# Expert weights in 2 MiB blocks: eight buffers of 4096 columns in place of sixteen of 2048

## The chip, the cores and the metric

The kernel runs on one core of a Trainium2 chip. The metric is the device time of one execution in microseconds (us), as the median of the runs shown. Shares, waits and durations come from one profiled execution, whose own time stands beside its span.

## What is computed

Two consecutive layers of a decoder trunk work on 256 tokens of width 1024, all in float32. Layer 0 has a hybrid mixer (gated linear attention beside sparse attention) and a dense SwiGLU. Layer 1 has a Mamba-2 mixer and eight SwiGLU experts of hidden width 3584, of which each token goes through the best two. A final norm follows. The part that most of the time goes to is this:

```python
def swiglu(h, w_gu, w_down):
    g, u = jnp.split(h @ w_gu, 2, axis=-1)
    return (jax.nn.silu(g) * u) @ w_down

def moe_ffn(h, router, w_gu, w_down):
    logits = (h @ router).astype(jnp.float32)
    top_val, top_idx = lax.top_k(logits, TOP_K)          # TOP_K = 2, N_EXPERTS = 8
    weights = jax.nn.softmax(top_val, axis=-1)
    gate = jnp.sum(jax.nn.one_hot(top_idx, N_EXPERTS) * weights[..., None], axis=-2)
    out = jnp.zeros(h.shape, jnp.float32)
    for e in range(N_EXPERTS):
        out = out + gate[..., e:e + 1] * swiglu(h, w_gu[e], w_down[e])
    return out
```

Every norm in front of a block is scaled and shifted by a projection of a vector `c` (1024 to 3072 columns per block). The weights of those projections are the "mod" weights below.

## The kernel before

**Stages.** From 0 to about 195 us the hybrid mixer runs, to about 375 us the dense SwiGLU, to about 610 us the Mamba-2 mixer, and from there to the end the experts. All matrix products of the first three stages are float32 products made of three: each block of weights is split into a high part (`wh`, ScalarE, line 252) and a low part (`wl`, VectorE, line 253), and TensorE multiplies high by high, high by low and low by high (lines 267 to 269). The split parts live in a ring of four slots of 1024 columns (pool `hl`). The mod weights of the next layers (`ssm_mod`, `moe_mod`) are multiplied and summed on VectorE (line 281, writing `junk`), as work between the splits of the dense stage.

**Loads.** All weights come through `load`: it takes a tile `raw` of 128 x 2048 float32 (1 MiB, 8192 bytes in a row per partition) and issues one DMA from the SP queue. The tiles come from pools that grow as room becomes free: six buffers at first, nine from the dense stage on, sixteen in the expert stage. A DMA into a buffer waits until the last reader of the block before is done, and the order on SP is fixed, so a DMA that waits holds up those behind it. The program has eight semaphores for SP's DMAs, and the ninth DMA waits until the first has landed: at most eight are under way. These waits are named DMAHW0 to DMAHW7 in the order of the program.

**Experts.** Each of the eight experts takes 42 blocks of 1 MiB, 352 MB in all. An expert's tokens are gathered into groups of 32 slots, three groups for the experts at even places and two for those at odd places, since the eight experts are worked through in an order that puts larger and smaller ones in turn. Its 3584 hidden columns are cut into chunks of 1024, 1024, 1024 and 512. For a chunk `gate_up` streams the weights `e_gu` (or `e_gl` for the short chunk) past the gathered tokens `gx`: one block of 1 MiB is one slice `k` of the contraction, and per group four matmuls of 32 rows by 512 columns run side by side on TensorE's column strips. Then SiLU (ScalarE, line 1470) and a product (VectorE, line 1471) write `sg`, `turn_a` transposes it to `at` (TensorE, line 1337), and `down` multiplies `at` by the blocks of `e_dn`. `scaled` multiplies an expert's result by its gate and splits it (`gate` on VectorE, `yh` on ScalarE, `yl` on VectorE, lines 1363 to 1365), and `scatter` adds it to the tokens (TensorE, line 1375). `gather` and `back` prepare the next two experts in between: `gather` is a generator that the loop advances by a step after the third yield of `gate_up` and after each SiLU.

**What sets the order.** The instructions are written in program order and then placed by a list scheduler, which estimates durations, puts what it expects to be ready first, and gives out the buffers. So another size of block also moves instructions on the compute engines, in the stages whose source lines are not touched too.

Of the kernel before, what the change touches and what calls it, by code (L numbers as in the profile page):

```python
# [8 lines left out]
F32 = mybir.dt.float32  # L9
# [7 lines left out]
D, T, KD = 1024, 256, 8  # L17
# [3 lines left out]
FE = 3584  # L21
NE = 8
# [81 lines left out]
def _layout(v):  # L104

    f = {k: np.asarray(a) for k, a in v.items()}
# [18 lines left out]
    for m in MODS:  # L125
# [51 lines left out]
    o["e_gu"] = eg.reshape(NE, 8, 128, 2, FE)[..., :3072].reshape(NE, 8, 128, 2, 3, 4, 256).transpose(  # L177
        0, 4, 1, 2, 5, 3, 6).reshape(NE, 3, 8, 128, 2, 1024)
    o["e_gl"] = eg.reshape(NE, 4, 2, 128, 2, FE)[..., 3072:].reshape(NE, 4, 2, 128, 2, 4, 128).transpose(
        0, 1, 3, 2, 5, 4, 6).reshape(NE, 4, 128, 2, 1024)  # L180
    o["e_dn"] = f["moe_w_down"][0].reshape(NE, 14, 2, 128, D).transpose(0, 1, 3, 2, 4)
# [4 lines left out]
def trunk_kernel(ctx: ExitStack, tc: tile.TileContext, d: dict, out: bass.AP):  # L186
    nc = tc.nc
# [5 lines left out]
    raw_p = ctx.enter_context(tc.tile_pool(name="raw", bufs=6))  # L193
# [27 lines left out]
    raws, hls = [(raw_p, 6)], []  # L221
# [11 lines left out]

    def load(ap):

        ap = ap.rearrange("p a b c -> p (a b c)") if len(ap.shape) == 4 else ap.rearrange("p a b -> p (a b)")
        r = ring("raw").tile([128, 2048], F32, name="raw")
        nc.sync.dma_start(r[:, :ap.shape[1]], ap)
        return r[:, :ap.shape[1]]
# [660 lines left out]
    raws.append((ctx.enter_context(tc.tile_pool(name="raw2", bufs=3, side="right")), 3))  # L900
# [286 lines left out]
    raws.append((ctx.enter_context(tc.tile_pool(name="raw3", bufs=7, side="right")), 7))  # L1187
    with ExitStack() as mx:
# [124 lines left out]
        def gate_up(e, c):  # L1313

            w = CHUNKS[c] // 2
            ps = [pbank("pa") for _ in range(NGS[e])]
            n = 512 // w
            for i in range(KD // n):
                blk = load(weights(e, d["e_gu"], c, i) if n == 1 else weights(e, d["e_gl"], i))
                for q in range(n):  # L1320
                    k = n * i + q
                    for r in range(NGS[e]):
                        strips(ps[r], [(gx[:, e % 4, k, r * NS:(r + 1) * NS],
                                        blk[:, (4 * q + j) * w:(4 * q + j + 1) * w]) for j in range(4)],
                               k == 0, k == KD - 1)
                yield ps
# [14 lines left out]
        def down(e, c, at, py):  # L1341
            m = CHUNKS[c] // 512
            n = NGS[e]

            def part(blk, f, r, h):
                j, f_ = divmod(f, m)
                o_ = f % 2 * D + h * 512
                return at[:, r * m + f_, 32 * j:32 * j + 32], blk[:, o_:o_ + 512]

            for i in range(2 * m):  # L1350
                blk = load(weights(e, d["e_dn"], 4 * c + i))
                for f in (2 * i, 2 * i + 1):
                    strips(py[0], [part(blk, f, r, h) for r in range(2) for h in range(2)],
                           c == 0 and f == 0, c == 3 and f == 4 * m - 1)
                if n == 3:
                    strips(py[1], [part(blk, f, 2, h) for f in (2 * i, 2 * i + 1) for h in range(2)],
                           c == 0 and i == 0, c == 3 and i == 2 * m - 1)
# [140 lines left out]
        def final():  # L1498
            xf = ring("raw").tile([128, 2048], F32, name="raw").rearrange("p (b n) -> p b n", b=2)
# [22 lines left out]
        with tc.If(nmax > 0):  # L1522
# [10 lines left out]
            with tc.For_i(0, NE, 1) as e:  # L1533
                for base in (0, 128):
# [23 lines left out]
                    for f0 in range(0, FE, 512):  # L1558
                        c, h_ = divmod(f0, 1024)
                        pgu = [pbank("pa") for _ in range(2)]  # L1560
                        for k in range(KD):
                            if c < 3:
                                r = load(d["e_gu"][bass.ds(e, 1), c, k].rearrange("a p k n -> p a k n"))
                                rk_ = r.rearrange("p (j u n) -> p u j n", j=4, u=2)[:, :, h_ // 256:h_ // 256 + 2]
                            else:
                                if k % 2 == 0:
                                    r = load(d["e_gl"][bass.ds(e, 1), k // 2].rearrange("a p k n -> p a k n"))
                                rk_ = r.rearrange("p (k j u n) -> p k u j n", k=2, j=4, u=2)[:, k % 2]
                            for u in range(2):
                                PE.matmul(pgu[u].rearrange("p (j n) -> p j n", n=rk_.shape[3]), g2[:, k], rk_[:, u],  # L1570
                                          start=k == 0, stop=k == KD - 1)
# [11 lines left out]
                        for f in range(4):  # L1583
                            if f % 2 == 0:
                                r = load(d["e_dn"][bass.ds(e, 1), f0 // 256 + f // 2].rearrange("a p k n -> p a k n"))
                            for n in range(2):
                                PE.matmul(py[n], at[:, f * 128:(f + 1) * 128],
                                          r[:, (f % 2) * D + n * 512:(f % 2) * D + n * 512 + 512],
                                          start=f0 == 0 and f == 0, stop=f0 == FE - 512 and f == 3)
# [28 lines left out]
```

## Time and profile before

| | us |
|---|---|
| median of 3 runs | 1457.8 (1455.94 to 1460.75) |
| profiled execution, its time | 1462.21 |
| its span, first to last instruction | 1460.3 |
| TensorE busy | 1416.4 (97% of the span) |
| VectorE busy | 562.3 (39%) |
| ScalarE busy | 436.2 (30%) |
| matmuls of the expert stage (line 1303), busy | 507.7 and 253.0 |
| bytes read from HBM | 490.70 MB |

The profile's page has the busy time of each engine, the span in 40 slices with the DMA rate in each, the chain of work that ended last, and the costliest groups of instructions with what ended the idle time before them. The rest is asked of the trace: waits by engine, windows, the chain in order of time, and a timeline of single instructions. A busy TensorE is not proof that it computes all the time, since the ends of its matmuls are modelled. What shows that it waits are the starts.

### The profile page before, as it was taken

What the parts mean: (1) busy time and instruction counts of PE and PEld (TensorE: products, weight loads), DVE (VectorE), ACT (ScalarE), POOL (GpSimd) and SP (SyncE); (2) the same over time, 40 slices, a digit from 0 to 9 for tenths busy, and PEclk for the clock granted to TensorE, in tenths of its full rate; (3) what the DMA queues carried; (4) which work ended last, traced back from release to release, by engine and by line L of the source; (5) the groups of instructions that cost most, each with busy time, mean ns of one, the idle gap of its engine ahead of it and who ended that gap; (6) DMA issues with size and microseconds to landing.
All of it is one profiled execution on the core that took longest, in us unless ns stands there. A gap on an engine that the chain in (4) does not pass through costs nothing.

```text
span 1460.3 us, 28550 instructions
## 1 busy us (share of the span) xinstructions
PE 1416.4 (97%) x12241; PEld 807.4 (55%) x12241; DVE 562.3 (39%) x1100; ACT 436.2 (30%) x854; POOL 5.3 (0%) x13
## 2 busy tenths in 40 slices
PE   6999999999999999999999999999999999999995
PEld 6866799999799987633433333333334333333331
DVE  7898688875678778511010011010100110100102
ACT  5577554444567685211100011000001000000001
POOL 0000000000000000000000000000000000000000
PEclk9999999999999999899999999999999999999998
DMA  9876788985544434799899999999999999999994
GB/s 383 347 287 251 298 297 333 366 312 210 229 145 160 158 116 144 288 362 369 336 410 421 419 420 420 419 421 420 420 420 420 420 421 420 420 420 420 420 420 161
DMA packets 68964, 493.66 MB, mean 338 GB/s; under 512 B 7648, under 2 KB 7904, under 8 KB 9568
## 3 DMA queue, kind: packets, MB, share of 16 engines
q1 hardware_dynamic: 68832, 491.77, 84.1%
q8 instruction: 98, 1.61, 0.4%
q14 instruction: 34, 0.28, 0.1%
HBM read 490.70 MB, written 1.05 MB: 337 GB/s over the span
## 4 chain that ended last, share of the span: by engine, by line
PE 93%; DVE 2%; DMA 2%; ACT 2%; issue 0%; SPq 0%; ACTq 0%; DVEq 0%
PE pa L1303 33%; PE pb L1303 16%; PE pa L267 7%; PE pa L268 7%; PE pa L269 7%; PE pb L268 3%; PE pb L269 3%; PE pb L267 3%; PE pc L1375 2%; PE pc L1337 1%; PE pc L1261 1%; DMA raw<-in_e_dn_dram 1%; PE pb L702 1%; DMA raw<-in_hyb_mod_dram 1%; ACT wh L252 1%; PE pa L732 1%
## 5 line engine op out<-in xcount | busy, mean ns | idle before, releaser
L1303 PE MATMUL pa<-raw,gx 128*32 128x512 f32 (+1 forms) x5120 | 507.7, 541 | 0.0
L1303 PEld LDWEIGHTS pa<-raw,gx 128*32 128x32 f32 x5120 | 166.9, 110 | 301.1 <-issue 262.0
L1303 PE MATMUL pb<-raw,at 128*32 128x512 f32 x2240 | 253.0, 594 | 2.2 <-DMA raw<-in_e_dn_dram 2.2
L1471 DVE TENSOR_TENSOR sg<-sg,pa 128x256 f32<-128x256 f32 (+1 forms) x80 | 31.0, 388 | 476.4 <-ACT sg L1470 474.7
L253 DVE TENSOR_TENSOR wl<-raw,wh 128x1024 fp32r<-128x1024 f32 (+1 forms) x155 | 185.5, 1205 | 58.4 <-ACT wh L252 58.2
L252 ACT CAST wh<-raw 128x1024 fp32r<-128x1024 f32 (+1 forms) x155 | 159.1, 1036 | 122.6 <-PE pb L268 52.9
L1303 PEld LDWEIGHTS pb<-raw,at 128*32 128x32 f32 x2240 | 70.5, 110 | 154.1 <-issue 144.2
L1470 ACT ACTIVATE sg<-pa 128x256 f32<-128x256 f32 (+1 forms) x80 | 28.6, 358 | 347.5 <-PE pa L1303 347.5
L267 PE MATMUL pa<-hh,wh 128*128 128x256 f32 (+1 forms) x392 | 113.4, 292 | 1.3 <-ACT hh L380 0.6
L268 PE MATMUL pa<-hl,wh 128*128 128x256 f32 (+1 forms) x392 | 112.7, 288 | 0.8 <-DVE hl L386 0.8
L269 PE MATMUL pa<-hh,wl 128*128 128x256 f32 (+1 forms) x392 | 112.6, 289 | 0.0
L267 PE MATMUL pb<-hh,wh 128*128 128x256 f32 (+1 forms) x360 | 101.9, 284 | 1.9 <-ACT hh L380 1.9
L268 PE MATMUL pb<-hl,wh 128*128 128x256 f32 (+1 forms) x360 | 102.5, 285 | 0.1
L269 PE MATMUL pb<-hh,wl 128*128 128x256 f32 (+1 forms) x360 | 102.2, 284 | 0.0
L1338 ACT COPY at<-pc 128x512 f32<-128x512 f32 (+2 forms) x32 | 17.5, 546 | 262.3 <-PE pb L1303 134.9
L281 DVE SCALAR_TENSOR_TENSOR junk<-raw,scb 128x1024 bf16<-128x1024 f32 x72 | 87.8, 1219 | 1.6 <-DMA raw<-in_hyb_mod_dram 1.0
L267 PEld LDWEIGHTS pa<-hh,wh 128*128 128x128 f32 (+1 forms) x392 | 74.9, 192 | 5.0 <-ACT wh L252 1.5
L268 PEld LDWEIGHTS pa<-hl,wh 128*128 128x128 f32 (+1 forms) x392 | 75.5, 193 | 2.1 <-DVE hl L386 0.9
L269 PEld LDWEIGHTS pa<-hh,wl 128*128 128x128 f32 (+1 forms) x392 | 75.3, 192 | 0.8 <-DVE gu L629 0.3
L267 PEld LDWEIGHTS pb<-hh,wh 128*128 128x128 f32 (+1 forms) x360 | 68.4, 190 | 2.9 <-ACT hh L380 2.1
L268 PEld LDWEIGHTS pb<-hl,wh 128*128 128x128 f32 (+1 forms) x360 | 68.7, 191 | 1.0 <-DVE hl L386 0.5
L269 PEld LDWEIGHTS pb<-hh,wl 128*128 128x128 f32 (+1 forms) x360 | 68.7, 191 | 0.3
(423 smaller groups left out, 1467.2 us busy)
## 6 DMA issues: line engine op xcount, KB each, us to landing
raw<-in_e_gu_dram SPq DMA_DIRECT2D x192, 1024.0 KB, 18.4
raw<-in_e_dn_dram SPq DMA_DIRECT2D x112, 1024.0 KB, 19.7
raw<-in_e_gl_dram SPq DMA_DIRECT2D x32, 1024.0 KB, 18.3
raw<-in_d_gu_dram SPq DMA_DIRECT2D x22, 1024.0 KB, 7.6
raw<-in_s_in_dram SPq DMA_DIRECT2D x20, 1024.0 KB, 4.8
raw<-in_hyb_mod_dram SPq DMA_DIRECT2D x12, 1024.0 KB, 9.6
raw<-in_ssm_mod_dram SPq DMA_DIRECT2D x12, 1024.0 KB, 6.6
raw<-in_d_dn_dram SPq DMA_DIRECT2D x11, 1024.0 KB, 7.3
```

Of the source, the lines that this page charges most:

```text
L252: hi_last[0] = S.copy(hi[:, :n], r)
L253: lo_last[0] = V.tensor_sub(lo[:, :n], r, hi[:, :n].bitcast(F32))
L267: PE.matmul(ps, a[0], b[0], start=start, stop=False, **kw)
L268: PE.matmul(ps, a[0], b[1], start=False, stop=False, **kw)
L269: return PE.matmul(ps, a[1], b[0], start=False, stop=stop, **kw)
L281: V.scalar_tensor_tensor(jk, r[:, q * D:(q + 1) * D], 1.0, scb, op0=OP.mult, op1=OP.mult, accum_out=macc[m][:, 2 * j + q:2 * j + q + 1])
L702: PE.matmul(pss[g], qbT[g * 64:(g + 1) * 64, r, q * 128:(q + 1) * 128], kT[g * 64:(g + 1) * 64, :, :n], start=True, stop=True)
L1303: up_last[0] = PE.matmul(ps[32 * j:32 * j + 32, :rhs.shape[1]], lhs, rhs, start=start, stop=stop)
L1338: (V.tensor_copy if i else S.copy)(at[:, i:i + n].rearrange("p a n -> p (a n)"), pt_[:, :n * 128])
L1375: PE.matmul(pso[b], at_place[e, q][:, h, b], p[:, q], start=i == 0, stop=i == 2 * n - 1)
L1470: last = act(sg[:, r, :w], pg[r][:, :w], AF.Silu)
L1471: V.tensor_mul(sg[:, r, :w], sg[:, r, :w], pg[r][:, w:2 * w])
```

## The change

The expert weights are laid out in blocks of 2 MiB: two slices of the contraction in one block of `e_gu`, four in one of `e_gl`, four row blocks in one of `e_dn`. A partition's row is 16384 bytes and contiguous. The buffers hold 4096 columns: three at first, four from the dense stage on, eight in the expert stage. Loads of up to 2048 columns, which is every load outside the experts, take half a buffer each: the first of two takes a new tile and the second takes its other half. The loops of `gate_up` and `down` walk the larger blocks in the same order of arithmetic, and `gate_up` yields after every second slice instead of each. The branch for tokens beyond the slots, which this input doesn't take, is changed alike and left out here.

```diff
     eg = f["moe_w_gu"][0]

-    o["e_gu"] = eg.reshape(NE, 8, 128, 2, FE)[..., :3072].reshape(NE, 8, 128, 2, 3, 4, 256).transpose(
-        0, 4, 1, 2, 5, 3, 6).reshape(NE, 3, 8, 128, 2, 1024)
-    o["e_gl"] = eg.reshape(NE, 4, 2, 128, 2, FE)[..., 3072:].reshape(NE, 4, 2, 128, 2, 4, 128).transpose(
-        0, 1, 3, 2, 5, 4, 6).reshape(NE, 4, 128, 2, 1024)
-    o["e_dn"] = f["moe_w_down"][0].reshape(NE, 14, 2, 128, D).transpose(0, 1, 3, 2, 4)
+    o["e_gu"] = eg.reshape(NE, 4, 2, 128, 2, FE)[..., :3072].reshape(NE, 4, 2, 128, 2, 3, 4, 256).transpose(
+        0, 5, 1, 3, 2, 6, 4, 7).reshape(NE, 3, 4, 128, 2, 2048)
+    o["e_gl"] = eg.reshape(NE, 2, 4, 128, 2, FE)[..., 3072:].reshape(NE, 2, 4, 128, 2, 4, 128).transpose(
+        0, 1, 3, 2, 5, 4, 6).reshape(NE, 2, 128, 4, 1024)
+    o["e_dn"] = f["moe_w_down"][0].reshape(NE, 7, 4, 128, D).transpose(0, 1, 3, 2, 4)
...
-    raw_p = ctx.enter_context(tc.tile_pool(name="raw", bufs=6))
+    raw_p = ctx.enter_context(tc.tile_pool(name="raw", bufs=3))
...
-    raws, hls = [(raw_p, 6)], []
+    raws, hls = [(raw_p, 3)], []
...
+    half = [None]
+
     def load(ap):

         ap = ap.rearrange("p a b c -> p (a b c)") if len(ap.shape) == 4 else ap.rearrange("p a b -> p (a b)")
-        r = ring("raw").tile([128, 2048], F32, name="raw")
-        nc.sync.dma_start(r[:, :ap.shape[1]], ap)
-        return r[:, :ap.shape[1]]
+        n = ap.shape[1]
+        if n <= 2048 and half[0] is not None:
+            r, half[0] = half[0], None
+        else:
+            r = ring("raw").tile([128, 4096], F32, name="raw")
+            half[0] = r[:, 2048:] if n <= 2048 else None
+        nc.sync.dma_start(r[:, :n], ap)
+        return r[:, :n]
...
-    raws.append((ctx.enter_context(tc.tile_pool(name="raw2", bufs=3, side="right")), 3))
+    raws.append((ctx.enter_context(tc.tile_pool(name="raw2", bufs=1, side="right")), 1))
...
-    raws.append((ctx.enter_context(tc.tile_pool(name="raw3", bufs=7, side="right")), 7))
+    raws.append((ctx.enter_context(tc.tile_pool(name="raw3", bufs=4, side="right")), 4))
...
-            n = 512 // w
+            n = 1024 // w
             for i in range(KD // n):
-                blk = load(weights(e, d["e_gu"], c, i) if n == 1 else weights(e, d["e_gl"], i))
+                blk = load(weights(e, d["e_gu"], c, i) if n == 2 else weights(e, d["e_gl"], i))
...
-                yield ps
+                    if k % 2 and k < KD - 1:
+                        yield ps
+            yield ps
...
-                o_ = f % 2 * D + h * 512
+                o_ = f % 4 * D + h * 512
                 return at[:, r * m + f_, 32 * j:32 * j + 32], blk[:, o_:o_ + 512]

-            for i in range(2 * m):
-                blk = load(weights(e, d["e_dn"], 4 * c + i))
-                for f in (2 * i, 2 * i + 1):
+            for i in range(m):
+                blk = load(weights(e, d["e_dn"], 2 * c + i))
+                for f in range(4 * i, 4 * i + 4):
                     strips(py[0], [part(blk, f, r, h) for r in range(2) for h in range(2)],
                            c == 0 and f == 0, c == 3 and f == 4 * m - 1)
-                if n == 3:
-                    strips(py[1], [part(blk, f, 2, h) for f in (2 * i, 2 * i + 1) for h in range(2)],
-                           c == 0 and i == 0, c == 3 and i == 2 * m - 1)
+                    if n == 3 and f % 2:
+                        strips(py[1], [part(blk, g, 2, h) for g in (f - 1, f) for h in range(2)],
+                               c == 0 and f == 1, c == 3 and f == 4 * m - 1)
```

In the dense stage on SP, around the seventh load of `ssm_mod` (a number behind a name tells one tile from another; what a row waits for is in brackets). Before, every load has a tile of its own:

```order
L238 DMA raw_2659<-in_d_gu_dram 128x2048 [waits DMAHW5_49]
L238 DMA raw_2725<-in_ssm_mod_dram 128x2048 [waits DMAHW6_49,DVE_49]
L238 DMA raw_2731<-in_ssm_mod_dram 128x2048 [waits DMAHW7_49,DMAHW3_49,DVE_49]
L238 DMA raw_2737<-in_ssm_mod_dram 128x2048 [waits DMAHW0_49,DVE_49,Activation_49]
L238 DMA raw_2743<-in_d_dn_dram 128x2048 [waits DMAHW4_49,DVE_49]
L238 DMA raw_2778<-in_d_gu_dram 128x2048 [waits DMAHW2_49,DVE_49,Activation_49]
L238 DMA raw_2845<-in_d_gu_dram 128x2048 [waits DMAHW6_49,DVE_49]
```

Now the same stretch has a tile for two loads, and the first of the two carries the wait for its buffer:

```order
L245 DMA raw_2527<-in_d_dn_dram 128x2048 [waits DVE_49]
L245 DMA raw_2527<-in_d_gu_dram 128x2048
L245 DMA raw_2699<-in_ssm_mod_dram 128x2048 [waits DMAHW2_49,DMAHW5_49,DMAHW1_49,DVE_49]
L245 DMA raw_2628<-in_d_gu_dram 128x2048 [waits DMAHW6_49,DVE_49,Activation_49]
L245 DMA raw_2628<-in_ssm_mod_dram 128x2048 [waits DMAHW7_49]
L245 DMA raw_2699<-in_ssm_mod_dram 128x2048 [waits DMAHW0_49]
L245 DMA raw_2710<-in_d_dn_dram 128x2048 [waits DVE_49]
L245 DMA raw_2710<-in_d_gu_dram 128x2048
L245 DMA raw_2811<-in_d_gu_dram 128x2048 [waits DMAHW3_49,DMAHW4_49,DVE_49,Activation_49]
```

The seventh load of `ssm_mod` (raw_2725 before, the second half of raw_2628 now) shares a buffer with a block of `d_gu`, and the eighth and ninth share raw_2699.

On VectorE in the same stretch, before, where `wl` is a split, `junk` the work on the mod weights, and `a` and `al` belong to the dense SwiGLU:

```order
L253 TENSOR_TENSOR wl_2409<-raw_2406,wh_2408 128x1024
L281 SCALAR_TENSOR_TENSOR junk_2727,mac_ssm_79<-raw_2725,scb_70 128x1024
L915 TENSOR_TENSOR a_2347<-sg_2345,pb_2286 128x256
L253 TENSOR_TENSOR wl_2437<-raw_2406,wh_2436 128x1024
L919 TENSOR_TENSOR al_2350<-a_2347,ah_2349 128x256
L281 SCALAR_TENSOR_TENSOR junk_2729,mac_ssm_79<-raw_2725,scb_70 128x1024
L253 TENSOR_TENSOR wl_2476<-raw_2473,wh_2475 128x1024
L281 SCALAR_TENSOR_TENSOR junk_2733,mac_ssm_79<-raw_2731,scb_70 128x1024
L253 TENSOR_TENSOR wl_2504<-raw_2473,wh_2503 128x1024
L281 SCALAR_TENSOR_TENSOR junk_2735,mac_ssm_79<-raw_2731,scb_70 128x1024
L253 TENSOR_TENSOR wl_2560<-raw_2557,wh_2559 128x1024
L281 SCALAR_TENSOR_TENSOR junk_2739,mac_ssm_79<-raw_2737,scb_70 128x1024
```

And now, beginning with the splits of the block of `d_dn` (raw_2527; raw_2557 before):

```order
L260 TENSOR_TENSOR wl_2530<-raw_2527,wh_2529 128x1024
L260 TENSOR_TENSOR wl_2546<-raw_2527,wh_2545 128x1024
L922 TENSOR_TENSOR a_2438<-sg_2436,pb_2378 128x256
L288 SCALAR_TENSOR_TENSOR junk_2695,mac_ssm_79<-raw_2628,scb_70 128x1024
L926 TENSOR_TENSOR al_2441<-a_2438,ah_2440 128x256
L288 SCALAR_TENSOR_TENSOR junk_2697,mac_ssm_79<-raw_2628,scb_70 128x1024
L260 TENSOR_TENSOR wl_2564<-raw_2527,wh_2563 128x1024
L288 SCALAR_TENSOR_TENSOR junk_2701,mac_ssm_79<-raw_2699,scb_70 128x1024
L922 TENSOR_TENSOR a_2505<-sg_2503,pb_2444 128x256
L260 TENSOR_TENSOR wl_2592<-raw_2527,wh_2591 128x1024
L926 TENSOR_TENSOR al_2508<-a_2505,ah_2507 128x256
L288 SCALAR_TENSOR_TENSOR junk_2703,mac_ssm_79<-raw_2699,scb_70 128x1024
```

The work on the seventh load stood between the two splits of a block of `d_gu` two blocks earlier, and stands now behind the two splits of the block of `d_dn`.

On TensorE in the expert stage, where an odd expert's last `down` ends and its first `scatter` begins, before:

```order
L1303 MATMUL pb<-raw,at 32x512 x16
L1303 MATMUL pa<-raw,gx 32x512
L1375 MATMUL pc<-yh,stT 128x512
L1375 MATMUL pc<-yl,stT 128x512
L1375 MATMUL pc<-yh,stT 128x512
L1375 MATMUL pc<-yl,stT 128x512
```

and now:

```order
L1310 MATMUL pb<-raw,at 32x512 x16
L1384 MATMUL pc<-yh,stT 128x512 x2
L1384 MATMUL pc<-yl,stT 128x512 x2
L1310 MATMUL pa<-raw,gx 32x512 x24
L1346 MATMUL pc<-cs,sg 128x128 x6
L1310 MATMUL pa<-raw,gx 32x512 x24
```

The two matmuls with `yh` now stand in front of the two with `yl`.

On TensorE in an even expert from the end of its second chunk's `gate_up` on (`pa`), with `gather` (`pc<-sr,xc`), `turn_a` (`pc<-cs,sg`) and `down` (`pb`), before:

```order
L1303 MATMUL pa<-raw,gx 32x512 x36
L1261 MATMUL pc<-sr,xc 128x160 x4
L1303 MATMUL pa<-raw,gx 32x512 x36
L1261 MATMUL pc<-sr,xc 128x160 x4
L1303 MATMUL pb<-raw,at 32x512 x48
L1303 MATMUL pa<-raw,gx 32x512 x12
L1337 MATMUL pc<-cs,sg 128x128 x6
L1303 MATMUL pa<-raw,gx 32x512 x24
L1261 MATMUL pc<-sr,xc 128x160 x2
```

and now:

```order
L1310 MATMUL pa<-raw,gx 32x512 x24
L1268 MATMUL pc<-sr,xc 128x160 x3
L1310 MATMUL pa<-raw,gx 32x512 x24
L1268 MATMUL pc<-sr,xc 128x160
L1346 MATMUL pc<-cs,sg 128x128 x3
L1310 MATMUL pb<-raw,at 32x512 x24
L1346 MATMUL pc<-cs,sg 128x128 x3
L1310 MATMUL pb<-raw,at 32x512 x24
L1268 MATMUL pc<-sr,xc 128x160
```

`turn_a` of the second chunk stood behind the whole `down` of the chunk before and the first slice of the next, and its first half now stands directly behind the last slices of its own chunk.

## Rows read from the trace of the kernel before

**Rows 1.** The page, span in 40 slices: DMA share in tenths, and rate.

```profile
DMA  9876788985544434799899999999999999999994
GB/s 383 347 287 251 298 297 333 366 312 210 229 145 160 158 116 144 288 362 369 336 410 421 419 420 420 419 421 420 420 420 420 420 421 420 420 420 420 420 420 161
```

**Rows 2.** Windows: stretch and length, then busy us of each engine, clock, DMA.

```profile
core 0: us, PE busy (x) PEld busy (x) DVE busy (x) ACT busy (x) POOL busy (x), PEclk, DMA share, GB/s
5.00:7.00 2.00, 0.00 (x0) 0.00 (x0) 0.16 (x1) 1.94 (x7) 0.00 (x0) 1.00 1.00 353
...
100.00:200.00 100.00, 98.42 (x647) 72.59 (x646) 77.47 (x165) 62.99 (x160) 1.45 (x4) 1.00 0.70 265
200.00:300.00 100.00, 100.00 (x707) 94.25 (x706) 84.06 (x119) 45.01 (x61) 0.00 (x0) 1.00 0.90 345
...
800.00:900.00 100.00, 98.80 (x936) 35.54 (x931) 10.76 (x24) 8.26 (x21) 0.00 (x0) 1.00 1.01 420
```

**Rows 3.** Waits of TensorE from 640 to 1445 us: total, times, longest.

```profile
PE pc L1375 <- ACT yh L1364: 3.6, 4, 1.5
PE pb L1303 <- DMA raw<-in_e_dn_dram: 2.2, 4, 0.7
```

**Rows 4.** Chain that ended last, experts: start us, us, what, count.

```profile
955.93 0.76 DVE gate L1363
...
956.71 0.63 ACT yh L1364
...
957.36 0.70 DVE yl L1365
...
977.21 0.39 ACT sg L1470
...
977.63 0.43 DVE sg L1471
...
1023.74 20.60 PE pa L1303 x192
...
1392.66 7.00 PE pb L1303 x64
```

**Rows 5.** Waits of SP, 640 to 840, then 1260 to 1461 us.

```profile
SPq L238 <- PE pa L1303: 78.6, 45, 4.3
SPq L238 <- DMA raw<-in_e_gu_dram: 25.3, 13, 2.0
...
SPq L238 <- DMA raw<-in_e_gu_dram: 67.9, 36, 3.0
...
SPq L238 <- PE pa L1303: 2.8, 8, 0.9
```

**Rows 6.** Timeline near the end: start us, us, engine, line, idle before.

```profile
1433.87 1.92 PE L1303 MATMUL pb<-raw,at 128*32 128x512 f32 x16 [0.54 <-DMA raw<-in_e_dn_dram]
...
1441.30 1.92 PE L1303 MATMUL pb<-raw,at 128*32 128x512 f32 x16 [0.46 <-DMA raw<-in_e_dn_dram]
```

**Rows 7.** Issue and first use of one block; landing times, 1000 to 1300 us.

```profile
1227.08 2.82 SPq L238 DMA_DIRECT2D raw<-in_e_dn_dram  x2
...
1252.86 3.62 PE L1303 MATMUL pb<-raw,at 128*32 128x512 f32 x32
...
raw<-in_e_dn_dram SPq DMA_DIRECT2D x38, 1024.0 KB, 19.8
```

**Rows 8.** Dense stage: timelines of SP and VectorE, then a group, a landing.

```profile
216.84 6.99 SPq L238 DMA_DIRECT2D raw<-in_ssm_mod_dram  x3
...
225.97 1.22 DVE L281 SCALAR_TENSOR_TENSOR junk<-raw,scb 128x1024 bf16<-128x1024 f32 x1
...
227.60 1.22 DVE L253 TENSOR_TENSOR wl<-raw,wh 128x1024 fp32r<-128x1024 f32 x1
...
239.19 1.22 DVE L253 TENSOR_TENSOR wl<-raw,wh 128x1024 fp32r<-128x1024 f32 x1
...
L252 ACT CAST wh<-raw 128x1024 fp32r<-128x1024 f32 (+1 forms) x155 | 159.1, 1036 | 122.6 <-PE pb L268 52.9
...
raw<-in_ssm_mod_dram SPq DMA_DIRECT2D x12, 1024.0 KB, 6.6
```

More of the change, by code (lines that the diff above doesn't have):

```diff
@@ L1498, in final @@
         def final():
-            xf = ring("raw").tile([128, 2048], F32, name="raw").rearrange("p (b n) -> p b n", b=2)
+            xf = ring("raw").tile([128, 4096], F32, name="raw")[:, :2048].rearrange("p (b n) -> p b n", b=2)
             h0, h1 = slice(0, 512), slice(512, D)
@@ L1562, in trunk_kernel @@
                             if c < 3:
-                                r = load(d["e_gu"][bass.ds(e, 1), c, k].rearrange("a p k n -> p a k n"))
-                                rk_ = r.rearrange("p (j u n) -> p u j n", j=4, u=2)[:, :, h_ // 256:h_ // 256 + 2]
-                            else:
-                                if k % 2 == 0:
-                                    r = load(d["e_gl"][bass.ds(e, 1), k // 2].rearrange("a p k n -> p a k n"))
-                                rk_ = r.rearrange("p (k j u n) -> p k u j n", k=2, j=4, u=2)[:, k % 2]
+                                if k % 2 == 0:
+                                    r = load(d["e_gu"][bass.ds(e, 1), c, k // 2].rearrange("a p k n -> p a k n"))
+                                rk_ = r.rearrange("p (k j u n) -> p k u j n", k=2, j=4, u=2)[
+                                    :, k % 2, :, h_ // 256:h_ // 256 + 2]
+                            else:
+                                if k % 4 == 0:
+                                    r = load(d["e_gl"][bass.ds(e, 1), k // 4].rearrange("a p k n -> p a k n"))
+                                rk_ = r.rearrange("p (k j u n) -> p k u j n", k=4, j=4, u=2)[:, k % 4]
                             for u in range(2):
@@ L1583, in trunk_kernel @@
                         for f in range(4):
-                            if f % 2 == 0:
-                                r = load(d["e_dn"][bass.ds(e, 1), f0 // 256 + f // 2].rearrange("a p k n -> p a k n"))
+                            if f == 0:
+                                r = load(d["e_dn"][bass.ds(e, 1), f0 // 512].rearrange("a p k n -> p a k n"))
                             for n in range(2):
                                 PE.matmul(py[n], at[:, f * 128:(f + 1) * 128],
-                                          r[:, (f % 2) * D + n * 512:(f % 2) * D + n * 512 + 512],
+                                          r[:, f * D + n * 512:f * D + n * 512 + 512],
                                           start=f0 == 0 and f == 0, stop=f0 == FE - 512 and f == 3)
```

## Prediction, before the changed kernel was run

> **What bounds the kernel now.** I read the page's 40 slices first. The DMA share is 9 tenths from slice 17 on and the rate stands at 420 GB/s through the whole expert stage [rows 1], with a share of 1.01 in a window of it [rows 2]. 420 GB/s is 2.50 us for 1 MiB. That alone says: bound by loads, so a larger load should help. The second view is what speaks against it. In the same window TensorE is busy for 98.80 of 100 us [rows 2], and in the stage's 800 us it waits for `e_dn` loads for 2.2 us in all [rows 3]. The chain gives TensorE's own pace: an even expert's 192 `gate_up` matmuls, eight slices of 24, take 20.60 us, which is 2.58 us for each 1 MiB; an odd expert's 64 `down` matmuls, four blocks, take 7.00 us, 1.75 us for each [rows 4]. So TensorE is slower than the stream in even experts and faster in odd ones. Over a pair of 84 blocks it needs about 42 × 2.58 + 42 × 1.75 = 182 us, with some 13 us per expert for transposes, gather, scatter and projection rows besides (the stage's 831 us less 4 × 182, over eight experts), so near 208; the stream needs 84 × 2.50 = 210. The sixteen buffers fill in even experts and drain in odd ones. SP's waits show it: from 640 to 840 us it stands for 78.6 us behind TensorE (no free buffer) and 25.3 behind loads; from 1260 us for 67.9 behind loads and 2.8 behind TensorE [rows 5]. The two are balanced to a per cent, and only at the very end does the stream come last: the final block's matmuls start 7.43 us after those of three blocks before (1441.30 less 1433.87, [rows 6]), where three blocks at TensorE's own 1.75 are 5.25.
>
> Before 610 us other things bound it: TensorE is busy 100.00 of 100 us in the dense stage, with loads at a share of 0.90, and 98.42 in the hybrid stage, share 0.70 [rows 2].
>
> **The change part by part. The stream.** What the last blocks still wait, 7.43 − 5.25 = 2.2 us, plus the 0.54 in front of the first of them [rows 6], is 2.7 us, and no faster stream gives back more than that, as TensorE paces the rest. How much faster is the stream? No row shows a row of 16 KiB. At 8 KiB each of 16 engines spends 8192 × 16 / 420 GB/s = 312 ns on a row. At the program's start, when the constants come in (rows of 1.4 to 4 KB by their shapes, 3.5 KB taken as the mean), the rate is 353 GB/s at a share of 1.00 [rows 2], so 162 ns a row. A straight line through both gives 579 ns for 16 KiB, 453 GB/s, the upper bound; the lower bound is 420 GB/s, since some of the difference at the start may be ramp and not row. I take 427, nearer the 8 KiB row. The gain counts only where SP waits for loads and not for a buffer, from 840 us at the latest [rows 5]: 1.7% of 600 us is 10 us. Against it stand 2.7 us to be removed, and the block's size: a block of 2 MiB is usable 2.5 us after its first half is now, and the last one has 3.5 us of TensorE behind its landing in place of 1.75. 2.7 + 2.5 + 1.75 = 7.0 is less than 10, so with 427 the wait goes in full: **−2.7 us**. Late next is TensorE itself.
>
> The page "DMA: Bandwidth & Descriptors" of the Trainium skill (section "Rules for kernel authors") asks for 128 partitions and at least 1 MiB for full bandwidth, which the loads already have, and its section "Specifications" puts the ceiling at 435 GB/s; by it the stream would have at most 3.5% left. The trace agrees in so far as nothing in it moves faster than 421; that 2 MiB brings more than 1 MiB no row here shows.
>
> **Starvation inside the stream.** One block of `e_dn` is issued at 1227.08 and first used at 1252.86, with landings of 19.8 us: 6 us in hand, the least that I found [rows 7]. A larger block takes 2.5 us (landing) and 2.6 us (release) of that, 5.1; a stream 1.7% faster has by then gained 0.017 × (1250 − 840) = 7.0. I take 0.
>
> **TensorE's order in the experts.** Larger blocks have fewer yields, and the scheduler places small work anew. Three places: (a) `scatter` of an odd expert now runs both `yh` matmuls ahead of both `yl`. `gate`, `yh` and `yl` take 0.76, 0.63 and 0.70 us in a row [rows 4], and TensorE's waits for `yh` are 3.6 us over four experts [rows 3]; the matmul that now stands in front covers at most 0.44 of `yl`, at three experts: −0.6 to −1.3, I take −0.9. (b) The first half of `turn_a` stands directly behind its own chunk's last slices in even experts, at eight places. `sg` needs ScalarE 0.39 and VectorE 0.43 us [rows 4], 0.8 together after the slices' end; the first of three groups ends a slice's third, 0.86 us, earlier than the next, so the wait is 0 to 0.9 at each place; I take near the lower end, +1.0 in all. (c) `back`'s small copies stand behind `sg` at three places, 0 to 1 us each: +1.0. Sum of the order: **+1.1**, bounds −1.3 and +9.
>
> **The early stages.** Two loads now share a buffer, which is free only when both are read, and three buffers of two replace six. TensorE has at most 1.6 us idle per 100 in the hybrid stage and 0.0 in the dense one [rows 2], so there is next to nothing to gain. The place at risk is in the first order above: the seventh `ssm_mod` load shares a buffer with `d_gu`. The slot's last reader before it is the split at 227.60 + 1.22 = 228.8; two loads, the second of them landing in some 6.6 to 7.6 us, make it ready at about 236, where its VectorE work began at 225.97 before [rows 8]. But that work was moved behind the two splits of `d_dn`, the second of which ended at 240.4 [rows 8]: 4 us in hand. If VectorE did stand there, the splits behind it would wait; the `hl` ring holds four parts, and 52.9 of the 122.6 us that ScalarE is idle ahead of its splits end with TensorE giving one back [rows 8], so the ring is often full and covers some of it. I take **0**, bounds 0 and +5.
>
> **Sum.** 1462.2 (the profiled execution's own time) − 2.7 + 1.1 + 0 = 1460.6; 1.6 below. On the median of the runs, 1457.8, that is **1456.2 us**. About 0.3%, 4.4 us, is what a measurement of this kernel can tell from no change.
>
> **The rivals.** *The stream is no faster.* At 420 GB/s the larger block is pure granularity: the last landing comes up to 2.6 us later, since its buffer was given back later, and its matmuls take 3.5 in place of 1.75. With the order's +1.1 that is 2.6 + 1.75 + 1.1 = +5.4: 1463, slower. For it: a share of 1.01 at 8 KiB looks like engines without gaps [rows 2]. Against: rows at the start take more than their bytes' share. It decides where the rate in the window 800 to 900 us stays under 423, where 0.7% of 600 us just pays 2.5 + 1.75. Chance 0.13.
>
> *The early loads come late.* Where the 4 us of the dense stage aren't there and TensorE runs out of split parts, it stands two or three times for 2 us: +5, 1461 to 1464. For it: no room behind 100.00 busy. Against: the cover worked out above. Chance 0.13.
>
> *The stream's gain is paid in full.* If TensorE's busy time hides waits, because its matmuls' ends are modelled, 1.7% of 839 is 14 us: 1443. Against it: even experts' 2.58 us is longer than the stream's 2.50, SP stands behind TensorE, and TensorE's waits are 2.2 us. The skill's same page, section "Measured", has 425 GB/s for its largest load; by that the stream would be 10 us shorter, and the time so only if the stream was the bound. Chance 0.05.
>
> *Order and waits do better than I reckon* (the scheduler removes waits of TensorE on `yh`, `sg` and loads beyond my sum, −4.5 to −7): 1451 to 1453. The visible waits on `yh` and `e_dn` are 5.8 us in all [rows 3], so most would have to go. Chance 0.13.
>
> *The change does nothing*: what it gains at the end it loses at the small transposes, within 1 us of 1457.8. Chance 0.10.
>
> **How the numbers follow.** The forecast itself (1453.6 to 1459) has 0.46. Faster by over 0.3% (below 1453.4): 0.05 + 0.13, and 0.01 of the forecast's edge, 0.19. Slower by over 0.3% (above 1462.2): two thirds of the two slow rivals, 0.17, and 0.04 for both together with (b) at its upper end: 0.21. Same: 0.60. The range leaves out the stream paid in full (0.05) and the far ends of the better order and of the slow rivals (some 0.1): 1451.5 to 1463.
>
> **What would show it.** The stream: the rate at 800 to 900 us at 424 or more; TensorE's waits on `e_dn` gone, the last three blocks' starts 5.25 us apart per 3 MiB, and SP behind TensorE after 1260 us too. The order: waits of TensorE on `sg` at line 1346 above today's, on `yl` at 1384 gone. The early stages: VectorE's waits on `ssm_mod` loads between 200 and 330 us, and TensorE below 100.00 in the window 200 to 300; stages should end within 1 us of today. I am wrong at the first step if the rate rises and the time falls by more than 5 us: then TensorE was not the bound that its starts make it.

## The result, and the profile after

The changed kernel takes 1471.9 us (median of 4 runs, 1468.6 to 1473.6) where the kernel before took 1458.8 in the same comparison: a ratio of 1.0084, 95% interval 1.0063 to 1.0104. It is 13 us slower. Forecast were 1456.2 us and a range of 1451.5 to 1463.0; the result lies outside it, on the other side. The profiled execution of the changed kernel took 1468.6 us, span 1466.6.

The stream did what was expected of it. The page's row of rates, and windows of the trace (columns as in [rows 2]):

```profile
GB/s 382 316 290 266 258 241 317 379 316 246 260 117 164 167 129 115 335 384 369 329 428 427 427 426 425 375 428 427 426 427 402 382 427 427 427 426 423 424 427 104
```

```profile
200.00:300.00 100.00, 100.00 (x717) 94.44 (x716) 83.43 (x120) 47.63 (x66) 0.00 (x0) 1.00 0.84 330
...
800.00:900.00 100.00, 96.84 (x902) 33.45 (x898) 10.85 (x24) 8.24 (x20) 0.00 (x0) 1.00 1.01 427
```

Beside [rows 1] and [rows 2], the rate in full stretches went from 420 to 427 GB/s, and it now dips (375, 402, 382) where it never dipped before. In the window of 800 to 900 us TensorE is busy for less, 96.84 in place of 98.80. SP's waits, 640 to 840 us and then 1260 to 1475, correspond to [rows 5]:

```profile
SPq L245 <- PE pa L1310: 111.2, 27, 7.6
SPq L245 <- PE pb L1310: 66.3, 14, 8.7
...
SPq L245 <- PE pa L1310: 95.0, 21, 7.7
SPq L245 <- PE pb L1310: 40.5, 9, 5.3
```

SP waits for no load any more: it stands behind TensorE to the end, so the dips in the rate are TensorE giving its buffers back late. TensorE's own waits from 640 us on (total, times, longest), to be read beside [rows 3], are below. No load is among them, and they are what shows that the stream is now ahead and TensorE sets the experts' time:

```profile
PE pc L1384 <- ACT yh L1373: 8.1, 7, 1.5
PE pc L1346 <- DVE sg L1480: 4.1, 11, 0.4
PE pc L1268 <- DVE at L1347: 1.6, 3, 0.5
PE pc L1290 <- DVE at L1347: 1.6, 3, 0.5
PE pc L1268 <- ACT gx L1272: 1.6, 2, 0.8
```

The waits for `e_dn` are gone, as forecast. But the waits of `scatter` for `yh` are 8.1 us where they were 3.6, and `gather` (line 1268) and `back` (line 1290) wait 4.8 us for tiles they hardly waited for before. From the first to the last expert matmul (line 1303 before, 1310 after) it was 609.9 to 1443.2, 833.3 us, and is 609.5 to 1449.6, 840.1 us. That the experts begin at the same time in these two traces is chance: TensorE's clock stood at 1.2 GHz for some 14 us around 600 in the profiled execution before, and for 3.4 us after, as windows of 2 us show. The experiments below take that apart.

**One scatter, before and after.** The timeline of TensorE at the end of an odd expert, before (start, length, engine, line, what, and in brackets the idle time in front and its releaser):

```profile
837.41 1.89 PE L1303 MATMUL pb<-raw,at 128*32 128x512 f32 x14
839.11 1.02 PE L1303 MATMUL pa<-raw,gx 128*32 128x512 f32 x2
840.82 0.50 PE L1375 MATMUL pc<-yh,stT 128*128 128x512 f32 x1 [0.69 <-ACT yh L1364]
841.55 0.50 PE L1375 MATMUL pc<-yl,stT 128*128 128x512 f32 x1 [0.22 <-DVE yl L1365]
```

and after, with VectorE and ScalarE among the rows:

```profile
836.63 2.76 PE L1310 MATMUL pb<-raw,at 128*32 128x512 f32 x24
...
839.46 0.75 DVE L1372 SCALAR_TENSOR_TENSOR gate<-pb,gs,gate 128x512 f32<-128x512 f32 x1 [2.60 <-PE pb L1310]
840.24 0.62 ACT L1373 CAST yh<-gate 128x512 fp32r<-128x512 f32 x1 [3.84 <-DVE gate L1372]
840.89 0.69 DVE L1374 TENSOR_TENSOR yl<-gate,yh 128x512 fp32r<-128x512 f32 x1 [0.68 <-ACT yh L1373]
...
840.91 0.73 PE L1384 MATMUL pc<-yh,stT 128*128 128x512 f32 x2 [1.53 <-ACT yh L1373]
```

Before, TensorE did a piece of the next expert's `gate_up` while `gate` and `yh` were made, and then stood for 0.69 + 0.22. After, nothing stands between the last `down` and `scatter`, and TensorE waits for the whole chain, 0.75 + 0.62 and the handovers: 1.53 us. The sum of the waits in a pair of experts, all read so, is 0.42 + 0.29 + 0.69 + 0.22 + 0.42 = 2.0 us in the pair up to 1000 us before. After it is 0.42 + 0.29 + 0.79 (gather) + 1.53 (scatter) + 0.55 (gather) + 0.55 (back) + 0.67 (scatter at the even expert's end) + 0.42 = 5.2.

### The profile page after: what moved, and what is told of

It is laid out like the page before. It is cut to its first block, busy times and chain, and to the rows that moved or that the text cites. A ratio compares the mean times of both kernels' runs of the same rounds, so it can differ in the third digit from the quotient of the medians.

```text
span 1466.6 us, 27878 instructions
## 1 busy us (share of the span) xinstructions
PE 1413.8 (96%) x12241; PEld 802.5 (55%) x12241; DVE 561.2 (38%) x1100; ACT 436.2 (30%) x854; POOL 5.3 (0%) x13
## 4 chain that ended last, share of the span: by engine, by line
PE 92%; DVE 3%; ACT 2%; issue 1%; DMA 1%; SPq 0%; ACTq 0%; DVEq 0%
PE pa L1310 34%; PE pb L1310 17%; PE pa L274 7%; PE pa L275 7%; PE pa L276 7%; PE pb L275 3%; PE pb L276 3%; PE pb L274 3%; PE pc L1384 2%; PE pc L1268 1%; PE pc L1346 1%; DMA raw<-in_hyb_mod_dram 1%; PE pa L739 1%; DVE junk L288 1%; PE pb L709 1%
## 5 line engine op out<-in xcount | busy, mean ns | idle before, releaser
(423 smaller groups left out, 1461.3 us busy)
```

## The experiments

The theories were: (1) TensorE's new order makes it wait, in the experts and at the end of the hybrid stage; (2) larger blocks cost by their granularity; (3) the shared buffers of the early stages cost. All runs side by side (e1 to e4 ran on one chip, e5 to e8 on a second, e9 on a third, each beside the kernel before; ratio to the kernel before on the same chip, with its interval; the clock is the mean granted clock over a kernel's runs; "at 0.990" reads each kernel's own runs at that clock from a straight line of time over clock, which falls by 8 to 10 us for each 0.01; the stretch is from the first to the last expert matmul of the profiled execution, and the kernel before has one, in the first row):

| kernel | median us (runs) | ratio | clock | at 0.990 | experts' stretch |
|---|---|---|---|---|---|
| before, beside e1 to e4 | 1459.8 (35) | | 0.990 | 1459.9 | 833.3 |
| before, beside e5 to e8 | 1459.1 (22) | | 0.990 | 1459.3 | |
| before, beside e9 | 1458.7 (9) | | 0.991 | 1459.0 | |
| changed, first comparison | 1471.9 (4) | 1.0084 [1.0063, 1.0104] | 0.987 | | 840.1 |
| e7 changed, again | 1474.6 (6) | 1.0091 [1.0062, 1.0121] | 0.985 | 1469.4 | 839.6 |
| e1 changed, order by hand | 1461.7 (12) | 1.0011 [0.9993, 1.0029] | 0.987 | 1458.0 | 827.1 |
| e2 before, order by hand | 1462.3 (12) | 1.0011 [0.9993, 1.0029] | 0.988 | 1459.6 | 832.9 |
| e3 changed, yields as before | 1467.5 (12) | 1.0049 [1.0028, 1.0069] | 0.985 | 1463.0 | 833.2 |
| e4 before, coarse yields | 1460.6 (12) | 1.0002 [0.9983, 1.0021] | 0.990 | 1461.3 | 835.7 |
| e5 shared buffers only | 1471.3 (6) | 1.0074 [1.0044, 1.0103] | 0.986 | 1466.2 | 834.2 |
| e6 change in the experts only | 1468.6 (11) | 1.0080 [1.0052, 1.0107] | 0.988 | 1468.1 | 840.3 |
| e8 both losses undone | 1456.1 (12) | 0.9974 [0.9953, 0.9995] | 0.989 | 1455.2 | 826.7 |
| e9 as e8, rows of 8 KiB | 1466.8 (5) | 1.0060 [1.0046, 1.0073] | 0.988 | | 837.5 |

**The order by hand, at 2 MiB and at 1 MiB (e1, e2).** Two edits on the changed kernel, and the same two on the kernel before: `turn_a` and both halves of `scatter` go behind the first slices of the next chunk.

```diff
                 if prev:
-                    at = turn_a(prev[0], prev[2], CHUNKS[prev[1]] // 4)
+                    with tc.issue_after(up_last[0].ins):
+                        at = turn_a(prev[0], prev[2], CHUNKS[prev[1]] // 4)
                 if y is not None:
+                    with tc.issue_after(up_last[0].ins):
+                        scatter(y[0], y[1], 0)
                     next(up)
-                    scatter(y[0], y[1], 1)
+                    with tc.issue_after(up_last[0].ins):
+                        scatter(y[0], y[1], 1)
                     y = None
...
                         y = pe_, scaled(pe_, py_)
-                        scatter(pe_, y[1], 0)
```

> The changed kernel, blocks of 2 MiB, with TensorE's small expert work put by hand: turn_a and both halves of scatter are placed behind the first slices of the next chunk, so that a scatter never stands directly behind down. Theory 1 (the loss is TensorE's order, as the expert pairs' waits went from 2.0 to 5.2 us each, and some 4 us at the end of the hybrid stage): TensorE's waits after 600 us fall from 21.5 us to 5 to 8, and the time from 1471.9 to 1456 to 1460. Theory 2 (the large blocks cost by their granularity): waits of TensorE stay or turn into waits on loads, 1468 to 1472. Theory 3 (the loss is in the early stages' shared buffers): 1466 to 1470, and the early part unchanged.

> The kernel before, blocks of 1 MiB, with the same placement by hand. Theory 1: TensorE's waits on yh, yl and sg, 9 us of 13.9, mostly go; but its own time for a pair is then some 206 us against 210 for a stream of 420 GB/s, so that the waits on e_dn at the end grow from 2.2 to 4 to 7 us, and the time falls by 2 to 5 us: 1453 to 1457. If the placement has a price of its own (another buffer held longer), 1459 or more.

TensorE's waits from 640 us on, in e1:

```profile
PE pb L1310 <- DMA raw<-in_e_dn_dram: 8.3, 8, 1.3
PE pa L1310 <- DMA raw<-in_e_gl_dram: 2.8, 4, 1.4
PE pa L1310 <- DMA raw<-in_e_gu_dram: 2.7, 2, 1.4
PE pc L1384 <- ACT yh L1373: 1.5, 1, 1.5
```

and in e2:

```profile
PE pb L1303 <- DMA raw<-in_e_dn_dram: 8.3, 15, 0.7
PE pa L1303 <- DMA raw<-in_e_gl_dram: 3.4, 6, 0.7
PE pa L1303 <- DMA raw<-in_e_gu_dram: 2.6, 5, 0.7
PE pc L1375 <- ACT yh L1364: 1.5, 1, 1.5
```

The waits for `yh`, `sg`, `at` and `gx` went to 2 us, the last scatter's mostly, which nothing can cover. In e1 the experts' stretch fell from 840 to 827 us: theory 1 for the experts, though the time, 1461.7, ended 1.7 us over what it expected. Two things had not been foreseen. With TensorE free of those waits the loads are the bound at either size of block: 13.8 us of waits for loads in e1 (8.3 + 2.8 + 2.7), 14.3 in e2. So at 1 MiB the order by hand gained nothing (832.9 beside 833.3; e2's 1462.3 missed the expected 1453 to 1457), and at 2 MiB the same edit gives 827.1: the faster stream is worth 5.8 us of the stretch, but only once TensorE no longer stands for other reasons. And e1 is not faster than the kernel before although its experts are 6 us faster, so something outside the experts costs about as much.

The waits are not all that the order changes. From the changed kernel to e1 TensorE's waits from 640 us on fall only from 18.3 to 16.1 us in all, since waits for loads came in place of the others, and yet the stretch falls by 13.0. Most of the rest shows in TensorE's changes between kinds of matmul. By the starts in the traces, waits left out, a small matmul (`pc`) behind an expert matmul starts 0.52 us after it, an expert matmul behind a small one 0.20, and one of `down` behind one of `gate_up`, or the reverse, 0.41 (medians), where expert matmuls of one kind follow each other every 0.09 to 0.10. All these changes together take 80.1 us before, 76.1 in the changed kernel, 67.3 in e1 and 73.3 in e2; TensorE goes over to small matmuls 106 times in the changed kernel and 72 times in e1. In the changed kernel's timeline, two expert matmuls alone between small ones take as long as eight in a row:

```profile
842.30 1.06 PE L1310 MATMUL pa<-raw,gx 128*32 128x512 f32 x8
...
959.71 1.05 PE L1310 MATMUL pa<-raw,gx 128*32 128x512 f32 x2
```

**The yields (e3, e4).** `gate_up` hands control back after each slice as before (e3), or after every second slice in the kernel before (e4). In the full chunks this shifts by up to four slices the point at which `gather` and `scatter` are called.

```diff
e3, on the changed kernel:
-                    if k % 2 and k < KD - 1:
+                    if (k + 1) % (512 // w) == 0:
                         yield ps
-            yield ps
e4, on the kernel before:
-                yield ps
+                if n > 1 or i % 2:
+                    yield ps
```

> The changed kernel with gate_up's yields as before (after each slice of 1 MiB), so that gather and scatter are called where they were. By the program's order scatter still stands directly behind down. Theory 1: only the waits of gather (3.6 us on sr) go, scatter's stay: 1467 to 1470. If the yields alone set the order's loss: 1459 to 1463. Theory 2: 1471 or more.

> The kernel before with gate_up's yields after every second slice, as in the change; loads, blocks and buffers as before. Theory 1: slower by the waits that the coarser yields bring, 2 to 6 us: 1461 to 1465, stream at 420 GB/s. Theories 2 and 3: within 1.5 us of the kernel before, 1457 to 1460.

TensorE's waits in e3, from 640 us on:

```profile
PE pc L1383 <- ACT yh L1372: 8.1, 7, 1.5
...
PE pc L1268 <- DVE at L1346: 0.5, 1, 0.5
```

e3's stretch is 833.2, so the yields are 6.9 us of the 13.0 between the changed kernel and e1, more than expected. 2.7 of the 6.9 show as waits of TensorE (`gather` and `back`, behind `at`), and the changes between kinds of matmul take 2.7 less, 73.4 in place of 76.1; the last 1.5 were not found. The waits for `yh` are 8.1 us in e3 too, and the time is 7.7 over the kernel before. In e4 the same coarse yields cost 2.4 us of the stretch, with more changes of matmul (85.4 us in place of 80.1) and not with more waits, and nothing measurable of the time. So neither the yields nor the size of the blocks alone is the whole: with blocks of 2 MiB `scatter` stands directly behind `down` whatever the yields are, and with blocks of 1 MiB it doesn't.

**The two halves of the change apart (e5, e6, e7).** e5 is the kernel before with `load` of the change, a buffer of 4096 columns for two loads everywhere, and expert blocks of 1 MiB as before. e6 is the change with early tiles of 2048 columns, six and nine of them, whose room is given back at the start of the experts to eight tiles of 4096. The edits, cut:

```diff
e5, on the kernel before:
-        r = ring("raw").tile([128, 2048], F32, name="raw")
+        if half[0] is not None:
+            r, half[0] = half[0], None
+        else:
+            r = ring("raw").tile([128, 4096], F32, name="raw")
+            half[0] = r[:, 2048:]
e6, on the changed kernel:
+        r = ring("raw").tile([128, 2048 if n <= 2048 else 4096], F32, name="raw")
...
+    rx.close()
+    raws[:] = [(ctx.enter_context(tc.tile_pool(name="raw3", bufs=8, side="right")), 8)]
```

> The kernel before with the shared buffers alone: two loads of 1 MiB to a buffer of 4096 columns in all stages, expert blocks still 1 MiB. TensorE's order is that of the change up to the experts, and that of the kernel before in the experts. If the early stages' new order costs what the traces showed at the end of the hybrid mixer (idle from 130 to 195 us 2.6 in place of 1.0, and about as much hidden in busy time), the time is 2 to 4 us over the kernel before: 1462 to 1464, with the experts unchanged at 833 us. If the early stages cost nothing: 1459 to 1461.

> The change in the experts alone: early loads keep a buffer of 2048 columns each (six and nine), and eight buffers of 4096 columns take their room in the expert stage. TensorE's order up to the experts is that of the kernel before, and from the third expert on that of the change. If the experts' order is most of the loss: 1465 to 1469, the experts' stretch 838 to 841 us where it was 833. If the early stages are most of it: 1460 to 1462.

> The changed kernel once more, in as many runs as the others, so that time and granted clock can be set side by side: median 1469 to 1473. At a mean clock of 0.990, by the slope of the runs of the kernel before, 1468 to 1469.

Both halves are slower by themselves. e6 has the whole loss of the experts (840.3) with the early stages as before, as expected. e7 repeats the first comparison, a little above what was expected (1474.6 for 1469 to 1473, and 1469.4 at 0.990). e5 has the experts as before (834.2) and is slower all the same, by 12 us in the median and 6.9 at equal clock, where 2 to 4 was expected. So theory 3 holds beside theory 1, but not by loads that come late: in the changed kernel's trace VectorE waits for a mod load between 200 and 330 us once, for 0.5 us, and TensorE is busy for 100.00 of 100 us there, as before. The loss lies ahead of it. At the end of the hybrid mixer, TensorE before:

```profile
177.52 0.38 PE L267 MATMUL pa<-hh,wh 128*128 128x256 f32 x1 [0.21 <-ACT hh L380]
178.26 0.71 PE L400 MATMUL pb<-dg,x 128*128 128x128 f32 x4 [0.35 <-DVE hf L385]
...
179.86 0.38 PE L267 MATMUL pa<-hh,wh 128*128 128x256 f32 x1 [0.41 <-ACT wh L252]
```

and after, TensorE and then VectorE:

```profile
178.87 0.71 PE L407 MATMUL pb<-dg,x 128*128 128x128 f32 x4 [0.49 <-DVE dg L397]
180.01 0.74 PE L274 MATMUL pa<-hh,wh 128*128 128x256 f32 x4 [0.43 <-ACT hh L387]
181.59 0.71 PE L407 MATMUL pb<-dg,x 128*128 128x128 f32 x4 [0.84 <-DVE hf L392]
183.06 0.39 PE L275 MATMUL pa<-hl,wh 128*128 128x256 f32 x1 [0.76 <-DVE hl L393]
...
178.73 2.35 DVE L260 TENSOR_TENSOR wl<-raw,wh 128x1024 fp32r<-128x1024 f32 x2
181.00 0.54 DVE L392 TENSOR_SCALAR hf<-pb,mac_dense 128x256 f32<-128x256 f32 x1
```

Two splits of weights, 2.35 us, now stand on VectorE ahead of `hf`, which TensorE waits for; the visible waits at this place are 2.5 us where they were 1.0. A second place shows hardly any wait (0.16 us). Around 140 us the same small matmuls stand in another order, before (e4, whose early order is that of the kernel before):

```profile
141.39 0.71 PE L829 MATMUL pb<-qa,ka 64*128 64x128 f32 x4
142.03 0.87 PE L732 MATMUL pa<-tT,vtok 128*64 128x256 f32 x8
...
143.64 0.71 PE L829 MATMUL pb<-qa,ka 64*128 64x128 f32 x8
...
144.71 0.87 PE L732 MATMUL pa<-tT,vtok 128*64 128x256 f32 x8
```

and after (e7):

```profile
141.75 0.65 PE L739 MATMUL pa<-tT,vtok 128*64 128x256 f32 x2 [0.16 <-ACT tT L735]
...
142.81 0.71 PE L836 MATMUL pb<-qa,ka 64*128 64x128 f32 x4
...
143.88 0.86 PE L739 MATMUL pa<-tT,vtok 128*64 128x256 f32 x6
...
145.15 0.71 PE L836 MATMUL pb<-qa,ka 64*128 64x128 f32 x6
145.79 0.92 PE L739 MATMUL pa<-tT,vtok 128*64 128x256 f32 x8
```

Groups of 4 and 8 matmuls became groups of 2, 4, 6 and 8: more changes from one shape to another, and two `tT,vtok` matmuls in 0.65 us where eight take 0.87. Matched matmul by matmul, e7 stands 0.13 us behind e4 at 138 us and 1.57 at 160, and goes from 1.59 to 2.95 across the place at 180; from there to the experts it stays at 2.9 to 3.0. The experts begin 3.0 us later in e7 than in e4 (615.7 and 612.7), and 3.5 later in e1 than in e8 below (616.0 and 612.5); up to there these four traces have the same six drops of TensorE's clock, alike in length and within some 7 us in place.

**Both losses undone (e8).** e6 with the order by hand of e1.

> Blocks of 2 MiB with TensorE's small expert work placed by hand as in e1, and the early loads with a buffer of 2048 columns each as in the kernel before, so that both losses are undone. If the two are all there is, what is left is the faster stream: the experts' stretch 826 to 829 us where it was 833, the early part as before, and 1453 to 1457 us, some 4 us under the kernel before. If large blocks have a price of their own: 1459 or more.

1456.1 us, ratio 0.9974 [0.9953, 0.9995]: as expected, and the only kernel here that is faster than the kernel before. Its blocks are of 2 MiB, so larger blocks as such (theory 2) are not the loss. e8 and e1 differ in the buffers alone (and so in when the experts' loads begin), and lie 5.5 us apart in the median, 2.8 at equal clock, on two chips where the kernel before differs by 0.7.

**Rows of 8 KiB in the same kernel (e9).** Each block of e8 is fetched by two DMAs of 1 MiB.

```diff
-        nc.sync.dma_start(r[:, :n], ap)
+        for o in range(0, n, 2048):
+            nc.sync.dma_start(r[:, o:min(n, o + 2048)], ap[:, o:min(n, o + 2048)])
```

> The kernel of e8 (own buffers early, TensorE's work in the experts placed by hand, buffers of 4096 columns), with each block of 2 MiB fetched by two DMAs of 1 MiB, so rows of 8192 bytes again. If the longer DMA row is what raised the stream from 420 to 427 GB/s: 420 in the windows between 1000 and 1400 us, the experts' stretch 831 to 834 us in place of 827, and 1459 to 1463 us. If it is the number of DMAs under way or the buffers: 427 and 1455 to 1458.

Windows of e8 and then of e9 (580 to 600 us, 1000 to 1200):

```profile
580.00:600.00 20.00, 19.29 (x102) 15.81 (x101) 11.77 (x25) 7.45 (x16) 0.00 (x0) 1.00 0.07 13
1000.00:1200.00 200.00, 197.16 (x1963) 70.77 (x1959) 21.60 (x50) 18.23 (x43) 0.00 (x0) 0.99 1.01 427
```

```profile
580.00:600.00 20.00, 19.28 (x111) 16.29 (x110) 11.19 (x26) 8.38 (x18) 0.00 (x0) 0.97 0.17 53
1000.00:1200.00 200.00, 196.40 (x1947) 69.54 (x1943) 21.71 (x50) 18.27 (x43) 0.00 (x0) 1.00 1.01 420
```

The rate falls back to 420 with buffers, places and TensorE's order (up to a few of `gather`'s matmuls) unchanged: the 427 come with the DMA of 2 MiB and its longer row, which this run doesn't tell from each other. The bytes under way are not the reason. In the changed kernel a block of 2 MiB lands 4.89 us after the one before with two or three blocks under way as with five; in e9 one of 1 MiB takes 2.48 with seven under way (medians from 640 us on). The time missed the expectation upwards, 1466.8 for 1459 to 1463. The late start explains it: in e8 and e9 the experts' loads can start only when the early tiles are given back, so little is fetched between 580 and 600 us, 53 GB/s in e9 where e2 had 171. When the experts begin, 4.2 MB of their blocks have landed in e9 and 12.6 in e2. e2's stream then stands for full buffers, and from 200 us into the experts on e9 is 2.1 MB behind e2 at the same distance, 5.0 us at 420; its stretch is 4.6 us over that of e2. With blocks of 2 MiB the late start costs nothing that shows: e1 has the early one (12.6 MB at the experts' beginning, e8 4.2), but 200 us on both have 88.1 MB, and their stretches are 827.1 and 826.7.

## Why the prediction was wrong, by its steps

**The stream: right.** 427 GB/s was taken, 427 came, and the waits of TensorE on `e_dn` (2.2 us) went. SP stands behind TensorE to the end too, but that sign tells nothing with eight buffers for at most eight DMAs under way: in e8, from 1000 to 1430 us, SP waits 331 us for TensorE and 5 for loads, while TensorE waits 13.0 for loads from 640 us on. The cap of 2.7 us on the gain was right for the kernel as it is: TensorE paces the rest. But the 208 us that TensorE was said to need for a pair were a quarter of the stage's 831, so they held its waits and its changes of matmul as if they were work. From the changed kernel to e1 its waits on other engines go from 18.3 to 2.3 us and its changes from 76.1 to 67.3. Freed of those, TensorE outruns both streams, and 2 MiB is worth 5.8 us.

**Starvation: right.** TensorE waits for no load of the experts in the changed kernel.

**TensorE's order in the experts, +1.1 us with bounds of −1.3 and +9: this step failed.** The stretch became 6.8 us longer while the stream gave some 2 back, so the order cost about 9, the far bound; TensorE's waits from 640 us on carry it, 10.9 us in all before and 18.3 after. (a) was reckoned at −0.9 because one more `yh` matmul stands in front of `yl`, and the waits for `yl` did go, 0.7 us in all. The row above it in the same listing was passed over: `pa<-raw,gx`, in front of the first `scatter` before, is gone. That piece of `gate_up` covered `gate` and `yh`, and without it the wait is 1.53 in place of 0.91. What stood in front was read for the matmuls that moved, and not for the work that was no longer there. (b), +1.0 for `turn_a` behind its own chunk, brought no more waits on `sg`: they are 4.1 us, 11 times, before and after; what is new stands behind its copies to `at`. (c), `back`, came out at 1.6 us for a reckoned 1.0, through those copies. `gather`, 3.2 us, was not reckoned, although its rows stand in the second listing, and neither was the even experts' `scatter`, 0.67 at each of three places. e3 sizes the parts: about 7 of the 9 hang on the yields, which call `gather`, `back` and `turn_a`, and about 2 are left for `scatter` behind `down`. Its waits grew by more than that, 3.6 to 8.1; that changes of matmul went with the missing piece of `gate_up` may make up for some of it, but was not measured apart.

**The early stages, 0 with bounds of 0 and +5: this step failed too.** The place examined, the mod loads in the dense stage, held. The cost lies in the hybrid stage and at its end, which were passed over with "next to nothing to gain", and the listing of those stages was not gone through. It is 3.0 to 3.5 us by traces with alike clock, by order and not by loads; e3, whose experts' stretch is that of the kernel before, is 3.1 us over it at equal clock. The rival "the early loads come late" came near the price by luck: its mechanism, VectorE waiting for mod loads, is not what happened.

**The clock, not in the sum at all.** The kernels with the early order of the change (the changed kernel in both comparisons, e1, e3, e5) ran at a mean granted clock of 0.985 to 0.987, those with the order of before (before itself, e2, e4, e6, e8, e9) at 0.988 to 0.991. The difference, 0.003, is about 3 us by the line of the runs. So at equal clock the changed kernel is some 10 us slower, and the rest of the 13 to 15 is clock. That the early order brings the lower clock is not shown: the groups all but touch, and the runs of one kernel spread over up to 0.013. The sum is then about 9 (order in the experts) − 2 (stream) + 3 (early order) + 3 (clock) = 13.

What stays open: e5 and e6 are 6.9 and 8.8 us over the kernel before at equal clock on their chip, 15.7 together, where the changed kernel (e7) is 10.1 over it. About 2 of the 5.6 us are seen: the stretch from the last expert matmul to the end is 17.1 us before and 17.0 after, 18.1 in e5 and 18.2 in e6. The rest was not followed up.

## What to carry to other kernels

Where two engines are balanced to a per cent, a faster stream gains only what the other leaves it, and the small waits of that other engine (here 2 to 5 us per pair of experts), with its changes from one kind of work to another, decide whether it shows. An edit of block sizes is also an edit of the order that a scheduler makes: go through the listing at every place where the bounding engine hands over to others, in all stages, and ask what stood in front of each dependent instruction before and no longer does. Where a wait appears, put independent work in front of it by hand, in few large pieces: with blocks of 2 MiB that turned 840 us into 827.

## What the runs showed of the hardware

A single DMA of 2 MiB with rows of 16 KiB streams 427 GB/s, two of 1 MiB with rows of 8 KiB 420, in otherwise the same kernel (e8, e9).

On TensorE a matmul on all 128 columns (`128*128`) behind one on a strip of 32 (`128*32`) starts 0.52 us after it, and one on a strip behind one on all columns 0.20 us (medians in the experts of the kernel before and the changed one, waits left out). No wait in the profile shows this time.

TensorE's clock fell after one of the three scatters between experts with the wait of 1.53 us in the profiled execution of the changed kernel, at 1052.37 us. Windows right behind it, the granted clock third from the end:

```profile
1053.00:1055.00 2.00, 2.00 (x11) 0.70 (x14) 1.32 (x3) 0.00 (x0) 0.00 (x0) 0.69 1.04 442
1055.00:1057.00 2.00, 2.00 (x12) 0.40 (x8) 0.00 (x0) 0.00 (x0) 0.00 (x0) 0.50 1.00 426
1057.00:1059.00 2.00, 2.00 (x24) 0.59 (x20) 0.00 (x0) 0.00 (x0) 0.00 (x0) 0.95 1.02 434
```

0.50 is 1.2 GHz of 2.4: TensorE was at the lower level for some 3.4 us and did 12 matmuls in 2 us in place of 24. The other two scatters with the same wait showed no drop, nor did the nine like them in e3, e6 and e7. Whether the wait brought the drop is not shown; it need not bring one. The runs of one kernel differ along with the clock: the 35 runs of the kernel before, 1455 to 1466 us, lie on a line of time over mean granted clock to within 1.2 us (standard deviation).
